# First modulation columns by float32 products with the weights stationary, and the first keys and queries summed by halves of the features

## Chip, core and metric

The program runs on one core of a Trainium2 chip. Its engines are TensorE (PE; loads of stationary operands are listed apart as PEld), VectorE (DVE), ScalarE (ACT), GpSimd (POOL) and SyncE (SP), which issues the transfers. Each engine works through its own list of instructions in order and waits on semaphores for the others. The metric is the device time of one launch in microseconds (us), lower is better. The kernel before took 2116.98 us, the median of three runs (2109.93 to 2120.24).

## What is computed

Two transformer blocks stand one behind the other. The change touches only the beginning of the first: the modulation of the inputs and the first keys and queries of its attention, cut here to this:

```python
def modulate(x, g, shift, scale):
    return rmsnorm(x, g) * (1 + scale) + shift

shift, scale, gate = jnp.split(jax.nn.silu(c) @ ada_w + ada_b, 3, axis=-1)
shift_c, scale_c, gate_c = jnp.split(jax.nn.silu(c_ctx) @ ada_w + ada_b, 3, axis=-1)
h = modulate(x, g_norm, shift[:, None], scale[:, None])
hc = modulate(ctx, g_norm, shift_c, scale_c)
y, yc = mixer_a(h, hc, ...)   # q, k, v, g = split(h @ w_in); rope; windowed attention with context keys
```

`x` has 512 tokens, `ctx` 256, both of 1024 features. `ada_w` is 1024 x 3072, and `c` and `c_ctx` are one vector each, so the modulation is a product of two rows with a large matrix: shift and scale are 2048 columns of it, for two vectors. All is float32.

## The kernel before, in words

Matrices are multiplied in float32 accuracy by splitting: `wchunk` loads a weight tile of 128 x 1024 (`raw`, 512 KB), ACT rounds it to `wH`, DVE forms the remainder `wL`, and three matmuls (H with H, L with H, H with L) stand for one product. A matmul of float32 operands that are not split is carried out by PE in two passes, and the trace counts each.

The start goes like this. `ada_stat` transposes the two condition vectors into `adast` (split, in a padded stationary operand) and `adafull` (float32, padded with zeros). `ada_cols` makes the modulation columns for one half of the features (`h`), first shift (`ada_b`), then scale (`ada_a`): `ada_chunk` sums over four weight tiles with the conditions stationary and 512 weight columns moving (tiles 0 and 2 split, 1 and 3 as float32), ACT brings the sum to `sgx`, and four products with `sel` turn its rows into columns in `tp`. In between, the six blocks of 128 tokens (two of context, four of x) are loaded (`load`), normalised and transposed (`turn`) into `xT`, features on partitions. When both halves of the columns are done, `modulate` applies them to the eight feature blocks: POOL and ACT do the context's, DVE and ACT the tokens', and both are split into X and Xc (`XH`, `XL`, `xcH`, `xcL`).

Then `attn_a` loads its constants, and `g_k(0)` and `g_q(0)` compute the first keys and queries with `gemm_T`: over the eight feature blocks k, three products each, for x (`px`, 512 columns) and context (`pc`, 256 columns). A rope, splits and copies by DMA follow, and `g_v`, the values, and the scores of the first head behind that.

The program text is written in terms of tiles; a scheduler puts each engine's instructions in order ahead of time and adds the semaphores. A tile name is reused when its last reader is done, and the transfer that refills it waits for that in SP's queue, with all that is issued behind it.

Of the kernel before, what the change touches and what calls it, by code (L numbers as in the profile page):

```python
# [270 lines left out]
class Prog:  # L271
# [193 lines left out]
    def ada_stat(self, th, ps):  # L465
        nc = self.nc
        tp = self.bank("tp")
        nc.tensor.transpose(tp[:, :16], th, self.ident[:16, :16])
        st = self.t(self.ap, [P, 8, 132], F32R, "adast", 1)
        nc.vector.memset(st.bitcast(F32), 0.0)  # L470
        v = tp[:, :16].rearrange("p (j k) -> p j k", j=2)
        for j in range(2):
            H, L = st[:, :, 3 + 64 * j], st[:, :, 35 + 64 * j]
            self.act(H, v[:, j])
            nc.vector.tensor_sub(L, v[:, j], H.bitcast(F32))
        self.adast = st
        full = self.t(self.np_, [P, 8, P], F32, "adafull", 1)
        nc.gpsimd.memset(full, 0.0)
        for j in range(2):
            nc.vector.tensor_copy(full[:, :, 64 * j], v[:, j])  # L480
        return full

    def ada_chunk(self, l, c, pm, row=0, full=None, fs=()):


        for i in range(4):
            if i in fs:
                raw = self.t(self.rp[0], [P, 1024], F32, "raw", self.rp[1])
                self.nc.sync.dma_start(raw, self.I[f"ada{l}"][c * 4 + i])
                for kk in range(2):  # L490
                    k = 2 * i + kk
                    self.mm(pm, full[:, k], raw[:, kk * 512:kk * 512 + 512], start=k == 0, stop=k == 7)
                yield
                continue
            HL = self.wchunk(self.I[f"ada{l}"][c * 4 + i])
            for kk in range(2):
                k = 2 * i + kk
                for w in range(2):
                    self.mm(pm, self.adast[:, k, 3 - row:131 - row], HL[w][:, kk * 512:kk * 512 + 512],
                            start=(k == 0 and w == 0), stop=(k == 7 and w == 1))  # L500
            yield
# [2 lines left out]
        self.ab = [self.t(self.ag if l else self.ap, [P, 2, 8], F32, f"ada_{n}{l}", 1) for n in "ab"]  # L504
        return self.ab

    def ada_cols(self, l, half, ps, tag, pool, full=None, fs=()):

        nc = self.nc
        a, b = self.ab  # L510
        hs = slice(4 * half, 4 * half + 4)
        bias = self.colv(f"ab{l}")
        for s_ in range(2):
            pm = self.bank(tag)
            yield from self.ada_chunk(l, 2 * s_ + half, pm, 0, full, fs)
            A = self.t(pool, [P, 512], F32, "sgx", 1)
            self.act(A, pm)
            tp = self.bank("tp")
            for f in range(4):
                self.mm(tp[:, 2 * f:2 * f + 2], A[:, f * P:(f + 1) * P], self.sel, start=True, stop=True)  # L520
            v = tp[:, :8].rearrange("p (k j) -> p k j", j=2)
            for j in range(2):
                bc = bias[:, 8 * s_ + 4 * half:8 * s_ + 4 * half + 4]
                if s_ == 0:
                    nc.vector.tensor_add(b[:, j, hs], v[:, :, j], bc)
                else:
                    g = self.colv(f"ng{l}")[:, hs]
                    nc.vector.tensor_add(a[:, j, hs], v[:, :, j], bc)
                    nc.vector.scalar_tensor_tensor(a[:, j, hs], a[:, j, hs], 1.0, g, op0=ALU.add, op1=ALU.mult)
            yield  # L530

    def ada_grow(self, l, c, ps, tag):
# [200 lines left out]
    def block1_(self):  # L733
# [3 lines left out]
        with ExitStack() as eb, ExitStack() as es:  # L737
# [5 lines left out]
            with ExitStack() as e2:  # L743
                tmp, ps = self.pool(e2, "A0"), None
                self.np_ = tmp
                th = self.ada_prep()
                full = self.ada_stat(th, ps)
                ab = self.ada_ab(0)
                self.rp = (tmp, 8)
                mm = "mm"  # L750
                xT = self.t(tmp, [P, 8, 768], F32, "xT", 1)

                def modulate(ks):
                    for k in ks:
                        for (j, sl, Z) in ((1, slice(0, C), Xc), (0, slice(C, C + S), X)):
                            x, a, b = xT[:, k, sl], ab[0][:, j, k:k + 1], ab[1][:, j, k:k + 1]
                            if j:
                                nc.gpsimd.tensor_scalar(x, x, a, b, op0=ALU.mult, op1=ALU.add)
                                self.act(Z[0][k], x)
                                nc.gpsimd.tensor_tensor(Z[1][k], x, Z[0][k].bitcast(F32), op=ALU.subtract)  # L760
                            else:
                                nc.vector.tensor_scalar(x, x, a, b, op0=ALU.mult, op1=ALU.add)
                                self.split(Z[0][k], Z[1][k], x)

                ga = chain(*[self.ada_cols(0, h, ps, mm, tmp, full, (1, 3)) for h in range(2)])

                def load(b):
                    xt = self.t(tmp, [P, D], F32, "x0", 6)
                    nc.sync.dma_start(xt, I["ctx"][b * P:(b + 1) * P] if b < 2 else I["x"][(b - 2) * P:(b - 1) * P])
                    return xt  # L770

                def turn(b, x):
                    r = self.row_r(x)
                    nc.vector.tensor_scalar(x, x, r, None, op0=ALU.mult)
                    for g in range(2):
                        tp = self.bank("mm", [P, 4, P])
                        for kk in range(4):
                            k = 4 * g + kk
                            nc.tensor.transpose(tp[:, kk, :], x[:, k * P:(k + 1) * P], self.ident)
                        dst = xT[:, 4 * g:4 * g + 4, b * P:(b + 1) * P]  # L780
                        if g == 0:
                            self.act(dst, tp)
                        else:
                            nc.vector.tensor_copy(dst, tp)

                run(some(ga, 1))
                for b in (0, 3):
                    xs = [load(b + i) for i in range(3)]
                    for i in range(3):
                        turn(b + i, xs[i])  # L790
                    run(some(ga, 3))
                run(ga)
                modulate(range(8))
                self.rp = None
            OT, OC = self.newO(), [self.oslot(k, F32) for k in range(8)]
            with ExitStack() as e2:
                self.attn_a(X, Xc, OT, OC, self.pool(e2, "A1"), None)
            if self.stop == "A1":
                for t in range(8):
                    self.dbg(f"OT{t}", OT[t])  # L800
# [65 lines left out]
            for b in range(4):  # L866
                self.dbg(f"x{b}", self.x[b])

    def attn_a(self, X, Xc, OT, OC, pool, ps):
        nc, I = self.nc, self.I  # L870
        rope = self.t(pool, [P, 2 * S], F32, "rope", 1)
        nc.sync.dma_start(rope, I["rope_a"])
# [4 lines left out]
        sink = self.bcast(I["a_sink"], pool, 16, "sink")  # L877
        nsink = self.t(pool, [P, 16], F32, "nsink", 1)
        nc.vector.tensor_scalar(nsink, sink, -1.0, None, op0=ALU.mult)
        V = [self.t(pool, [P, 4, P], F32R, f"V{b}", 1) for b in range(6)]  # L880
        K, Q, sg = {}, {}, {}

# [5 lines left out]
        def g_v():  # L888
            HL = [self.wchunk(I["a_v"][i]) for i in range(2)]
            for b in range(6):  # L890
# [8 lines left out]
                pv = pm[:, :256].rearrange("p (h d) -> p h d", h=4)  # L899
                self.split(V[b][:, :, 0:64], V[b][:, :, 64:128], pv)  # L900

        def g_k(pr):
            W = self.wchunk(I["a_k"][pr])
            px, pc, tk = toks()
            yield from self.gemm_T(W, tk)
            kf = self.rope(px, pool, rope, rot)
            kH = self.t(pool, [P, 768], F32R, "tH", 1)
            kL = self.t(pool, [P, 768], F32R, "tL", 1)
            self.split(kH[:, :C], kL[:, :C], pc[:, :C])
            self.split(kH[:, C:], kL[:, C:], kf)  # L910
            for e in range(2):
                k2 = self.t(pool, [P, 2, 768], F32R, "K", 2)
                for i, src in enumerate((kH, kL)):
                    for hf in range(2):
                        self.dcopy(k2[64 * hf:64 * hf + 64, i, :], src[64 * e:64 * e + 64, :])
                K[2 * pr + e] = k2
            yield

        def g_q(t):
            W = self.wchunk(I["a_q"][t])  # L920
            px, pc, tk = toks()
            yield from self.gemm_T(W, tk)
            qf = self.rope(px, pool, rope, rot)
            qH = self.t(pool, [P, 768], F32R, "tH", 1)
            qL = self.t(pool, [P, 768], F32R, "tL", 1)
# [7 lines left out]
            yield  # L933

        def g_g(t):
            W = self.wchunk(I["a_g"][t])
            px, pc, tk = toks()
            yield from self.gemm_T(W, tk)
            sg[t] = sx, sc = self.t(pool, [P, S], F32, "sgx", 1), self.t(pool, [P, C], F32, "sgc", 1)
            for ps_g, g in ((pc[:, :C], sc), (px, sx)):  # L940
                self.act(g, ps_g, AF.Tanh, scale=0.5)
                nc.vector.scalar_tensor_tensor(g, g, 1.0, ps_g, op0=ALU.add, op1=ALU.mult)
            yield
# [929 lines left out]
```

## Time and profile before

| what | us |
|---|---|
| median of three runs | 2116.98 |
| profiled execution, its own time | 2119.62 |
| its span | 2117.8 |
| PE busy in the span | 2032.1 (96%) |
| columns of the first half of the features ready | 35.3 |
| columns of the second half ready | 55.1 |
| first matmul of the first key sum | 51.87 |
| first matmul of V | 79.22 |

The span runs from the first to the last instruction of the profiled execution; 1.8 us of its time lie around it. A row of the timeline gives start, duration, engine, line and operation, then output<-inputs and their shapes, and in brackets how long the engine had been idle and what ended that. The duration of a matmul includes its way through the array, so its pace is the distance from one start to the next. PEclk is the share of TensorE's full clock (2.4 GHz) that was granted; 0.50 is 1.2 GHz.

### The profile page before, as it was taken

The page shows a single profiled execution, that of the slowest core. Times are in us where ns is not written, and L with a number is a line of the kernel's source. Part 1 is how long each engine was busy: PE and PEld are TensorE (multiplying, and loading weights), DVE is VectorE, ACT ScalarE, POOL GpSimd, SP SyncE. Part 2 cuts the span into 40 slices and gives each one's busy share as a digit, 9 for nine tenths or more (in the row PEclk, how much of TensorE's full clock was granted, in tenths as well). Part 3 has the DMA queues.
Part 4 walks back from the last instruction along what each step waited for, and adds up shares of the span by engine and source line. Part 5 has one row for each costly group of instructions (what it writes and reads, how often), then busy time and mean ns, then how long its engine had stood idle before and what let it go on. Part 6 is the DMA issues. An engine that isn't in the chain of part 4 may idle for free.

```text
span 2117.8 us, 28799 instructions
## 1 busy us (share of the span) xinstructions
PE 2032.1 (96%) x10609; PEld 1688.5 (80%) x10609; DVE 1293.2 (61%) x2491; ACT 1056.4 (50%) x2044; POOL 74.0 (3%) x162
## 2 busy tenths in 40 slices
PE   7899999998999999998999999999999999999998
PEld 4788888778788887876778888887888878888886
DVE  5588788846478886657756444423566775444323
ACT  5477677725367763555534333322466754333321
POOL 2100000000000000000000000000000000000000
PEclk9999999999999999999999999999999999999999
DMA  7344423322444332232223233232565533333332
GB/s 261 100 132 135 115 85 97 118 71 69 124 94 109 86 97 80 94 90 61 60 90 114 96 100 100 91 99 80 138 158 152 140 120 100 100 100 94 96 96 83
DMA packets 80893, 223.65 MB, mean 106 GB/s; under 512 B 13408, under 2 KB 19312, under 8 KB 80752
## 3 DMA queue, kind: packets, MB, share of 16 engines
q1 hardware_dynamic: 80752, 221.81, 34.8%
q8 instruction: 84, 1.38, 0.3%
q14 instruction: 57, 0.47, 0.1%
HBM read 176.67 MB, written 4.19 MB: 85 GB/s over the span
## 4 chain that ended last, share of the span: by engine, by line
PE 82%; DVE 7%; ACT 5%; issue 2%; DMA 2%; POOL 2%; SPq 0%; POOLq 0%; ACTq 0%; DVEq 0%
PE pj L293 33%; PE S L293 28%; PE po L293 13%; PE tp L293 2%; DVE wL L304 2%; PE tp L1305 2%; PE tp L1100 1%; ACT wH L290 1%; POOL rstd L336 1%; ACT tmp L290 1%; ACT junk L290 1%; DVE XL L584 1%; PE tp L375 1%; PE tp L1792 1%; ACT P L290 1%
## 5 line engine op out<-in xcount | busy, mean ns | idle before, releaser
L304 DVE TENSOR_TENSOR wL<-raw,wH 128x1024 fp32r<-128x1024 f32 (+2 forms) x291 | 354.1, 1221 | 465.4 <-ACT wH L290 453.2
L290 ACT ACTIVATE wH<-raw 128x1024 fp32r<-128x1024 f32 (+2 forms) x291 | 305.5, 1053 | 546.4 <-PE S L293 217.6
L293 PE MATMUL pj<-XH,wH 128*128 128x512 f32 (+1 forms) x672 | 259.9, 390 | 2.9 <-ACT tmp L290 1.5
L293 PE MATMUL pj<-XL,wH 128*128 128x512 f32 (+1 forms) x672 | 258.9, 389 | 0.1
L293 PE MATMUL pj<-XH,wL 128*128 128x512 f32 (+1 forms) x672 | 256.0, 384 | 0.5 <-DVE wL L304 0.5
L293 PE MATMUL S<-K,Q 96*128 96x384 f32 (+4 forms) x864 | 189.2, 329 | 3.9 <-ACT P L290 3.0
L293 PE MATMUL S<-XH,wH 128*128 128x512 f32 (+1 forms) x456 | 170.0, 373 | 1.0 <-ACT wH L290 1.0
L293 PE MATMUL S<-XH,wL 128*128 128x512 f32 (+1 forms) x456 | 170.1, 373 | 0.5 <-DVE wL L304 0.5
L293 PE MATMUL S<-XL,wH 128*128 128x512 f32 (+1 forms) x456 | 169.9, 373 | 0.0
L293 PEld LDWEIGHTS S<-K,Q 128*128 128x128 f32 (+1 forms) x864 | 140.7, 189 | 19.2 <-ACT P L290 7.3
L293 PEld LDWEIGHTS pj<-XH,wH 128*128 128x128 f32 x672 | 127.4, 190 | 28.5 <-ACT tmp L290 2.3
L293 PEld LDWEIGHTS pj<-XH,wL 128*128 128x128 f32 x672 | 127.0, 190 | 22.4 <-DVE wL L304 0.8
L293 PEld LDWEIGHTS pj<-XL,wH 128*128 128x128 f32 x672 | 127.1, 190 | 22.0 <-issue 0.4
L290 ACT ACTIVATE PTH<-tp 128x512 fp32r<-128x512 f32 (+2 forms) x192 | 91.3, 480 | 45.1 <-PE tp L1100 14.0
L584 DVE TENSOR_TENSOR PTL<-tp,PTH 128x512 fp32r<-128x512 f32 (+2 forms) x192 | 103.6, 543 | 10.2 <-ACT PTH L290 9.5
L293 PEld LDWEIGHTS S<-XH,wH 128*128 128x128 f32 x456 | 86.2, 189 | 16.6 <-ACT wH L290 1.7
L293 PEld LDWEIGHTS S<-XH,wL 128*128 128x128 f32 x456 | 86.2, 189 | 15.7 <-DVE wL L304 1.0
L293 PEld LDWEIGHTS S<-XL,wH 128*128 128x128 f32 x456 | 86.2, 189 | 15.2
L290 ACT ACTIVATE XH<-tp 128x512 fp32r<-128x512 f32 x128 | 75.1, 596 | 43.4 <-PE tp L375 24.0
L584 DVE TENSOR_TENSOR XL<-tp,XH 128x512 fp32r<-128x512 f32 x128 | 86.9, 686 | 10.6 <-ACT XH L290 9.5
L290 ACT ACTIVATE P<-S,nm 128x768 f32<-128x768 f32 (+1 forms) x96 | 72.5, 757 | 31.5 <-DVE nm L1018 12.4
L293 PE MATMUL po<-PTH,V 128*128 128x256 f32 (+1 forms) x224 | 78.8, 355 | 2.7 <-ACT PTH L290 2.3
(482 smaller groups left out, 4500.8 us busy)
## 6 DMA issues: line engine op xcount, KB each, us to landing
raw<-in_up SPq DMA_DIRECT2D x88, 512.0 KB, 3.5
raw<-in_ada SPq DMA_DIRECT2D x48, 512.0 KB, 4.2
raw<-in_dn SPq DMA_DIRECT2D x44, 512.0 KB, 3.5
raw<-in_o_o SPq DMA_DIRECT2D x11, 512.0 KB, 4.3
x<-in_x SPq DMA_DIRECT2D x8, 512.0 KB, 9.0
raw<-in_a_q SPq DMA_DIRECT2D x8, 512.0 KB, 4.7
raw<-in_a_g SPq DMA_DIRECT2D x8, 512.0 KB, 3.7
raw<-in_a_o SPq DMA_DIRECT2D x8, 512.0 KB, 3.6
```

Source lines behind the costliest of these rows:

```text
L290: self.nc.scalar.activation(out, in_, func, **kw)
L293: return self.nc.tensor.matmul(out, l, r, start=start, stop=stop, **kw)
L304: nc.vector.tensor_sub(L[:, :n], raw[:, :n], H[:, :n].bitcast(F32))
L336: self.nc.gpsimd.tensor_tensor(r, ms, self.c_mh[:, :n], op=ALU.pow)
L375: nc.tensor.transpose(tp[:, kk, :], xh[g][:, kk * P:(kk + 1) * P], self.ident)
L584: self.nc.vector.tensor_sub(L, src, H.bitcast(F32))
L1100: nc.tensor.transpose(tp[:, (i - i0) * P:(i - i0 + 1) * P], Ps[i][0][:, at(i) * P:(at(i) + 1) * P], self.ident)
L1305: nc.tensor.transpose(tp[:, i * P:(i + 1) * P], Ps[i][:, kb * P:(kb + 1) * P], self.ident)
L1792: nc.tensor.transpose(tp[:, (i - kb) * P:(i - kb + 1) * P], Ps[i][0][:, kb * P:(kb + 1) * P], self.ident)
```

## The change

The columns of layer 0 are no longer made by `ada_cols`. A new `ada_feat` loads the same tiles as plain float32 (those of the shift in halves, into the free tiles `OT`), makes each 128 x 128 piece of the weights the stationary operand and moves the two conditions (`cT`, two columns) past it; the sum over k stands in `tp` as columns at once. `ada_put` is the code that added bias and gain before. The six blocks of tokens are loaded ahead of all weights, and `turn` squares a whole row at a time. The constants of attention are loaded by `consts_a`, ahead of the second half's weights. The first key and query sums run as two generators, step by step: over the first four feature blocks when the first half is modulated, over the other four when the second is. The context is now modulated by ACT, not POOL. Layer 1 goes on as before.

```diff
+        cT = self.t(self.ap, [P, 8, 2], F32, "adac", 1)
+        nc.vector.tensor_copy(cT.rearrange("p k j -> p j k"), v)
...
+    def ada_feat(self, l, half, cT):
+        for s_ in range(2):
+            tp = self.bank("tp")
+            for i in range(4):
+                src = self.I[f"ada{l}"][(2 * s_ + half) * 4 + i]
+                if s_ == 0:
+                    raw = [self.t(self.op, [P, 512], F32, f"OT{2 * i + kk}", 1) for kk in range(2)]
+                    for kk in range(2):
+                        self.nc.sync.dma_start(raw[kk], src[:, kk * 512:kk * 512 + 512])
+                else:
+                    raw = self.t(self.rp[0], [P, 1024], F32, "raw", self.rp[1])
+                    self.nc.sync.dma_start(raw, src)
+                    raw = [raw[:, :512], raw[:, 512:]]
+                for kk in range(2):
+                    for f in range(4):
+                        self.mm(tp[:, 2 * f:2 * f + 2], raw[kk][:, f * P:f * P + P], cT[:, 2 * i + kk],
+                                start=i + kk + f == 0, stop=i == 3 and kk == 1, skip_group_check=True)
+                yield
+            self.ada_put(l, half, s_, tp)
+            yield
...
-                    r = self.row_r(x)
-                    nc.vector.tensor_scalar(x, x, r, None, op0=ALU.mult)
+                    ss = self.t(self.sm, [P, 2], F32, "ss2", 8)
+                    self.act(self.t(tmp, [P, D], BF16, "junkx", 1), x, AF.Square, scale=1.0 / 32.0, accum_out=ss[:, 0:1])
+                    nc.vector.tensor_scalar(ss[:, 0:1], ss[:, 0:1], EPS, None, op0=ALU.add)
+                    nc.vector.tensor_scalar(x, x, self.rstd(ss[:, 0:1]), None, op0=ALU.mult)
...
-                run(some(ga, 1))
-                for b in (0, 3):
-                    xs = [load(b + i) for i in range(3)]
-                    for i in range(3):
-                        turn(b + i, xs[i])
-                    run(some(ga, 3))
-                run(ga)
-                modulate(range(8))
+                def modulate(k):
+                    xs, zs = xT[:, k, C:], xT[:, k, :C]
+                    nc.vector.tensor_scalar(xs, xs, ab[0][:, 0, k:k + 1], ab[1][:, 0, k:k + 1], op0=ALU.mult, op1=ALU.add)
+                    self.act(zs, zs, scale=ab[0][:, 1, k:k + 1], bias=ab[1][:, 1, k:k + 1])
+                    self.split(X[0][k], X[1][k], xs)
+                    self.split(Xc[0][k], Xc[1][k], zs)
+
+                gas = [self.ada_feat(0, h, cT) for h in range(2)]
+                xs = [load(b) for b in range(6)]
+                for b in range(6):
+                    turn(b, xs[b])
+                    run(some(gas[0], 1))
+                run(gas[0])
+
+                Ws = [self.wchunk(I["a_k"][0]), self.wchunk(I["a_q"][0])]
+                consts = self.consts_a(self.pool(ea, "A0c", "right"))
+                begun = [[self.bank(kind) for _ in range(2)] for kind in ("pj", "S")]
+                gs = [self.gemm_T(W, [(X, S, px), (Xc, C, pc[:, :C])]) for W, (px, pc) in zip(Ws, begun)]
+                for h in range(2):
+                    for k in range(4):
+                        modulate(4 * h + k)
+                        for g in gs:
+                            run(some(g, 3))
+                        if h == 0:
+                            run(some(gas[1], 3 if k == 3 else 2))
+                    run(gas[1])
+                for g in gs:
+                    run(g)
...
         def g_k(pr):
-            W = self.wchunk(I["a_k"][pr])
-            px, pc, tk = toks()
-            yield from self.gemm_T(W, tk)
+            px, pc = begun[0] if pr == 0 else (yield from proj(I["a_k"][pr]))
```

PE's list in the kernel before, from the last column groups of the second half (`raw` by `adafull`) into the key sum (`pj_510`, `pj_511`):

```order
L293 MATMUL S_380<-wH_397,adast_113 128x512
L293 MATMUL S_380<-wL_398,adast_113 128x512
L293 MATMUL S_380<-raw_405,adafull_119 128x512 x2
L293 MATMUL pj_510<-XH_6_91,wH_506 128x512
L293 MATMUL pj_511<-xcH_10_95,wH_506 128x256
L293 MATMUL pj_510<-XL_8_93,wH_506 128x512
```

The key sum stood behind all products of the columns. PE's list in the changed kernel, at the end of the first half's columns (`tp_155` shift, `tp_301` scale) and the start of the key and query sums (`pj_371`, `pj_372` and `S_373`):

```order
L293 MATMUL tp_155<-adac_119,OT_56_250 128x2 x4
L293 MATMUL tp_301<-adac_119,raw_302 128x2 x8
L293 MATMUL tp_301<-adac_119,raw_312 128x2 x8
L293 MATMUL tp_301<-adac_119,raw_322 128x2 x8
L293 MATMUL tp_301<-adac_119,raw_332 128x2 x8
L293 MATMUL pj_371<-XH_6_91,wH_348 128x512
L293 MATMUL pj_371<-XL_8_93,wH_348 128x512
L293 MATMUL pj_372<-xcH_10_95,wH_348 128x256
L293 MATMUL pj_371<-XH_6_91,wL_349 128x512
L293 MATMUL S_373<-XH_6_91,wH_354 128x512
```

The key and query sums now stand behind the first half's columns alone, and the columns are made by matmuls of two moving columns. Further down in the same list, where the first half's sums go over into the second half's (`tp_393` and `tp_480` are the second half's columns, `XH_7` its features):

```order
L293 MATMUL S_374<-xcL_12_97,wH_354 128x256
L293 MATMUL S_373<-XH_6_91,wL_355 128x512
L293 MATMUL tp_393<-adac_119,OT_94_448 128x2 x4
L293 MATMUL S_374<-xcH_10_95,wL_355 128x256
L293 MATMUL tp_393<-adac_119,OT_95_449 128x2 x4
L293 MATMUL tp_480<-adac_119,raw_481 128x2 x8
L293 MATMUL tp_480<-adac_119,raw_509 128x2 x8
L293 MATMUL tp_480<-adac_119,raw_519 128x2 x8
L293 MATMUL tp_480<-adac_119,raw_529 128x2 x8
L293 MATMUL pj_371<-XH_7_92,wH_348 128x512
```

Half of the second half's column products stand among the sums over the first half, the other half between the two parts of the sums.

## Rows read from the trace of the kernel before

**Rows 1.** The page: busy time of each engine, its share of the span, instructions.
```profile
PE 2032.1 (96%) x10609; PEld 1688.5 (80%) x10609; DVE 1293.2 (61%) x2491; ACT 1056.4 (50%) x2044; POOL 74.0 (3%) x162
```
**Rows 2.** The chain that ended last: start, us, what.
```profile
35.09 0.23 DVE ada_a L528 x2
...
54.89 0.23 DVE ada_a L528 x2
```
**Rows 3.** Timeline of PE: keys, queries, and V's first matmul.
```profile
66.63 0.63 PE L293 MATMUL pj<-XL,wH 128*128 128x512 f32 x1
67.06 0.63 PE L293 MATMUL pj<-XH,wL 128*128 128x512 f32 x1
...
75.10 0.40 PE L293 MATMUL pj<-XH,wH 128*128 128x512 f32 x1
...
75.46 0.39 PE L293 MATMUL pj<-XL,wH 128*128 128x512 f32 x1
...
77.09 0.28 PE L293 MATMUL pj<-xcH,wL 128*128 128x256 f32 x1
...
79.22 0.68 PE L293 MATMUL pj<-wH,xcH 128*128 128x256 f32 x1
```
**Rows 4.** Windows: stretch and length, busy (instructions) by engine, PEclk, DMA share, GB/s.
```profile
90.00:100.00 10.00, 10.00 (x79) 9.64 (x79) 8.04 (x28) 6.85 (x19) 0.00 (x0) 1.00 0.01 2
```
**Rows 5.** Windows of PE alone: stretch and length, busy, PEclk, DMA share, GB/s.
```profile
25.00:25.50 0.50, 0.28 (x2) 1.00 1.00 401
25.50:26.00 0.50, 0.50 (x4) 0.58 1.01 401
...
29.00:29.50 0.50, 0.50 (x2) 1.00 0.75 303
```
**Rows 6.** Timeline of PE: transposes, and eight passes of two columns.
```profile
12.08 1.06 PE L779 MATMUL pj<-ident,x 128*128 128x128 f32 x4
12.94 1.91 PE L779 MATMUL S<-ident,x 128*128 128x128 f32 x8
...
16.71 0.60 PE L779 MATMUL po<-ident,x 128*128 128x128 f32 x4
17.15 0.60 PE L779 MATMUL pj<-ident,x 128*128 128x128 f32 x4
...
21.95 0.95 PE L293 MATMUL tp<-sel,sgx 128*128 128x2 f32 x8
```
**Rows 7.** Timeline of PE: matmuls of 160 columns, then of 416.
```profile
491.57 0.27 PE L293 MATMUL S<-wH,xcH 128*128 128x160 f32 x1
491.68 0.28 PE L293 MATMUL S<-wL,xcH 128*128 128x160 f32 x1
...
502.97 0.41 PE L293 MATMUL po<-wH,xcH 128*128 128x160 f32 x1
503.18 0.41 PE L293 MATMUL po<-wL,xcH 128*128 128x160 f32 x1
...
503.61 0.63 PE L293 MATMUL pj<-wH,XH 128*128 128x416 f32 x1
```
**Rows 8.** Windows of PE alone around that stretch.
```profile
497.00:498.00 1.00, 0.86 (x5) 0.50 0.67 249
...
506.00:507.00 1.00, 1.00 (x4) 0.57 0.07 16
```
**Rows 9.** Timeline of the other engines in the first 40 us.
```profile
6.23 1.06 ACT L290 ACTIVATE wH<-raw 128x1024 fp32r<-128x1024 f32 x1 [1.96 <-DMA raw<-in_ada]
...
8.26 0.63 ACT L290 ACTIVATE junk<-x 128x512 bf16<-128x512 f32 x1
8.79 0.19 ACT L290 ACTIVATION_READ_ACCUMULATOR junk<-x 128x1 f32 x1
...
9.31 0.55 POOL L336 TENSOR_TENSOR rstd<-ss,mh 128x1 f32<-128x1 f32 x1 [7.63 <-DVE adast L475]
9.90 0.75 DVE L774 TENSOR_SCALAR x<-x,rstd 128x1024 f32<-128x1024 f32 x1 [0.44 <-POOL rstd L336]
12.32 0.60 ACT L290 ACTIVATE xT<-S 128x512 f32<-128x512 f32 x1 [1.08 <-PE S L779]
...
35.49 1.55 DVE L762 TENSOR_SCALAR xT<-xT,ada_a,ada_b 128x512 f32<-128x512 f32 x3
36.96 1.21 DVE L304 TENSOR_TENSOR wL<-raw,wH 128x1024 fp32r<-128x1024 f32 x1
```
**Rows 10.** The tile `sgx`, first 70 us: count, ns min/median/max, first and last start, forms.
```profile
L293 PE MATMUL tp<-sel,sgx x32: 165/251/272, 22.0 to 54.6; 128*128 128x2 f32 x32
```

More of the change, by code (lines that the diff above doesn't have):

```diff
@@ L476, in ada_stat, with ada_chunk @@
         self.adast = st
[L477 to L483, printed above, removed]
-        for i in range(4):
[L487 to L494, printed above, removed]
+        cT = self.t(self.ap, [P, 8, 2], F32, "adac", 1)
+        nc.vector.tensor_copy(cT.rearrange("p k j -> p j k"), v)
+        return cT
+    def ada_feat(self, l, half, cT):
[18 more added lines that the diff above has]
+            yield
+    def ada_chunk(self, l, c, pm, row=0):
+        for i in range(4):
             HL = self.wchunk(self.I[f"ada{l}"][c * 4 + i])
@@ L505, in ada_ab, with ada_put @@
         return self.ab
-    def ada_cols(self, l, half, ps, tag, pool, full=None, fs=()):
+    def ada_put(self, l, half, s_, tp):
         nc = self.nc
@@ L511, in ada_cols @@
         hs = slice(4 * half, 4 * half + 4)
-        bias = self.colv(f"ab{l}")
+        v = tp[:, :8].rearrange("p (k j) -> p k j", j=2)
+        for j in range(2):
+            bc = self.colv(f"ab{l}")[:, 8 * s_ + 4 * half:8 * s_ + 4 * half + 4]
+            if s_ == 0:
+                nc.vector.tensor_add(b[:, j, hs], v[:, :, j], bc)
+            else:
+                g = self.colv(f"ng{l}")[:, hs]
+                nc.vector.tensor_add(a[:, j, hs], v[:, :, j], bc)
+                nc.vector.scalar_tensor_tensor(a[:, j, hs], a[:, j, hs], 1.0, g, op0=ALU.add, op1=ALU.mult)
+    def ada_cols(self, l, half, ps, tag, pool):
         for s_ in range(2):
             pm = self.bank(tag)
-            yield from self.ada_chunk(l, 2 * s_ + half, pm, 0, full, fs)
+            yield from self.ada_chunk(l, 2 * s_ + half, pm)
             A = self.t(pool, [P, 512], F32, "sgx", 1)
@@ L520, in ada_cols @@
                 self.mm(tp[:, 2 * f:2 * f + 2], A[:, f * P:(f + 1) * P], self.sel, start=True, stop=True)
[L521 to L529, printed above, removed]
+            self.ada_put(l, half, s_, tp)
             yield
@@ L746, in block1_ @@
                 th = self.ada_prep()
-                full = self.ada_stat(th, ps)
+                self.rp = (tmp, 8)
+                cT = self.ada_stat(th, ps)
                 ab = self.ada_ab(0)
-                self.rp = (tmp, 8)
-                mm = "mm"
                 xT = self.t(tmp, [P, 8, 768], F32, "xT", 1)
[L753 to L765, printed above, removed]
                 def load(b):
@@ L796, in block1_ @@
             with ExitStack() as e2:
-                self.attn_a(X, Xc, OT, OC, self.pool(e2, "A1"), None)
+                self.attn_a(X, Xc, OT, OC, self.pool(e2, "A1"), None, consts, begun)
             if self.stop == "A1":
@@ L867, in block1_, with consts_a @@
                 self.dbg(f"x{b}", self.x[b])
-    def attn_a(self, X, Xc, OT, OC, pool, ps):
+    def consts_a(self, pool):
         nc, I = self.nc, self.I
@@ L879, in attn_a @@
         nc.vector.tensor_scalar(nsink, sink, -1.0, None, op0=ALU.mult)
+        return rope, rot, mask, sink, nsink
+    def attn_a(self, X, Xc, OT, OC, pool, ps, consts, begun):
+        nc, I = self.nc, self.I
+        rope, rot, mask, sink, nsink = consts
         V = [self.t(pool, [P, 4, P], F32R, f"V{b}", 1) for b in range(6)]
@@ L900, in g_v, with proj @@
                 self.split(V[b][:, :, 0:64], V[b][:, :, 64:128], pv)
+        def proj(W):
+            px, pc, tk = toks()
+            yield from self.gemm_T(self.wchunk(W), tk)
+            return px, pc
         def g_k(pr):
-            W = self.wchunk(I["a_k"][pr])
-            px, pc, tk = toks()
-            yield from self.gemm_T(W, tk)
+            px, pc = begun[0] if pr == 0 else (yield from proj(I["a_k"][pr]))
             kf = self.rope(px, pool, rope, rot)
@@ L919, in g_q @@
         def g_q(t):
-            W = self.wchunk(I["a_q"][t])
-            px, pc, tk = toks()
-            yield from self.gemm_T(W, tk)
+            px, pc = begun[1] if t == 0 else (yield from proj(I["a_q"][t]))
             qf = self.rope(px, pool, rope, rot)
@@ L935, in g_g @@
         def g_g(t):
-            W = self.wchunk(I["a_g"][t])
-            px, pc, tk = toks()
-            yield from self.gemm_T(W, tk)
+            px, pc = yield from proj(I["a_g"][t])
             sg[t] = sx, sc = self.t(pool, [P, S], F32, "sgx", 1), self.t(pool, [P, C], F32, "sgc", 1)
```

## The prediction

> **What bounds the kernel now.** I read the page first: PE is busy for 96% of the span [rows 1], so a change near the start counts only as far as it lets PE reach its later work sooner or later. The chain of waits shows where the start is spent: the modulation columns of the first half of the features are ready at 35.3 us, those of the second half at 55.1 [rows 2]. After them come the sums of the first keys and queries. The timeline has their last matmul at 77.09 and the first matmul of V at 79.22 [rows 3], and from 90 to 100 PE has no idle time [rows 4]. Behind the first V matmul both programs issue the same work, and V's 144 matmuls give the ropes and copies of keys and queries time to finish. So the time changes by as much as the first V matmul moves. I call that moment M: 79.2 before.
>
> What the change puts ahead of M depends on the clock, so I looked at that next. It stood at full speed until 25.5 us and then fell to half until 29 [rows 5]. What PE had done just before the fall was transposes, eight passes of two columns [rows 6], and waits: it was busy for 0.28 of the last 0.50 us. The second place lies at 497 to 506 [rows 7, 8]: PE busy without a gap, with matmuls of 160 columns whose pace is not their streaming but the weight load; the clock stood at 0.50 all that time and rose only after matmuls of 416 columns. These two places decide the forecast.
>
> **What goes, what comes.** Before, each of four column groups took two weight tiles by eight matmuls of split weights and two by four float32 ones. Their eight splits each on ACT and DVE go (1.06 and 1.21 us [rows 9]), as do four evacuations and the two-column products behind them. Now all 128 products are float32 with the weights stationary and two columns moving; each is two passes, 256 in all. The trace has this operation, eight passes in 0.95 us at full clock [rows 6], one of them 0.25 [rows 10]: (0.95 - 0.25)/7 = 0.10 us a pass. At half clock the trace never shows it. From below its pace is 0.10, if the load does not follow the clock; from above 0.21, the pace of the 160-column matmuls at half clock (502.97 to 503.18) against 0.11 at full (491.57 to 491.68) [rows 7]. I take 0.21: both are paced by a 128-column weight load. So the 256 passes cost 26 us at full clock and 54 at half.
>
> *Until the first half is ready.* The first transfer in the queue is now x, not a weight tile. The one there before had landed by 6.23 [rows 9]; at 401 GB/s [rows 5] a 0.52 MB tile follows every 1.31 us, so the sixth x is there at 12.8. Two squares of 512 with their read (0.63 + 0.19 each [rows 9]) become one of 1024, not shown: at least 1.06 + 0.19 = 1.25 (the 1024-wide copy), at most 2 x 0.82 = 1.64; I take 1.25, since only the length changes. From a square's end to the first transpose takes 1.7 us (adds, the power on POOL 0.55, the scaling 0.75 [rows 9], and the steps between). So transposes begin at about 9.2. ACT has six squares and six 0.60 evacuations [rows 9], 11.1 us from 6.3, and the last square ends near 16.9: the last x is ready at 18.5. On PE a group of four transposes costs 0.86 at half clock and 0.44 at full [rows 6]. The first three x fill it to 14.4, the fourth is ready at 15.5. From there come 6 groups and 32 passes: all at half clock 5.2 + 6.7 = 11.9, until 27.4; all at full, held by the last x, 20.2. Before, transposes alone brought the clock up (half pace at 12.08, full at 16.71), so some run at full clock: I take 26. Then 96 passes in a row: 20.2 at half clock, 46.2. Four small DVE steps of 0.23 [rows 2] make it T = 47, against 35.3 before.
>
> *The sums over the first half, with the second half's first 64 passes between them.* DVE's modulation (1.55 for three [rows 9]), XH (0.60, as an evacuation of that size) and, queued behind it on ACT, the copy of the key weights (1.06) stand ahead of the first matmul: T + 2.3; the first product with wL waits for wL (1.21) to T + 4.2. PE has 24 pairs (a 512 and a 256 matmul), 0.35 a pair (75.10 to 75.46 [rows 3]): 8.3 us at full clock, double at half (66.63 to 67.06 is 0.43 for a 512 [rows 3]). 3.7 us of it (11 matmuls of 512, 10 of 256) come before the first two-column group in PE's order. They begin at half clock; dense work brought it back after 3.4 us in the fall at 25.6 [rows 5], so they end at about T + 9. The rest, 4.6 + 6.4 = 11.0 us at full clock, alternates dense matmuls and passes. If it falls again as at 25.6, 3.4 of it run at full and 7.6 take 15.2: T + 27.7. A mixed stretch like this is not in the trace; bounds are 11.0 and 22.
>
> *The last 64 passes* run by themselves, because the second half's matmuls in PE's order stand behind them: 13.4 at half clock, 6.4 at full; T + 41. Columns, modulation and XH: 2.4 us in which PE has nothing queued. The second half's 24 pairs: 8.3 + 1.7 for the clock's return. With 0.5 for the first rope M = T + 54 = 101.
>
> The other edits: the constants' loads move ahead in SP's queue past the second half's weights and are no longer late; POOL loses the context's modulation, and ACT and DVE take it over, which have room once those splits are gone. The loads of the second half wait in SP's queue for PE's passes to free their tiles, and V's weights are queued behind; at 401 GB/s and 54 us of PE work none of them comes late. I set these at nothing; they would cost up to 2 us if V's tiles were late.
>
> Sum: 101 - 79.2 = +22 us on the profiled execution's 2119.6, which stands 2.6 above the median; on the median 2139.
>
> The Trainium skill, TensorE: Matmul & The Clock Gate, section "What's actually happening", says that the half clock is the default state and activity releases it; the trace agrees at both places [rows 5, 8], and this speaks against the change.
>
> **Rivals.** *The clock stays at full* through the passes, because PE is never idle. For it: in the trace two-column passes came in eights only, and the fall at 25.6 had waits beside them. Against it: the 160-column stretch had none [rows 8]. Then T = 20.2 + 9.6 + 0.9 = 30.7, T + 9 less 1.5 for the sums begun warm, 11.0, 6.4, 2.4, 8.3 and 0.5 give M = 66.8: -12, 2105. This one is faster: it decides from the point at which fewer than some 40% of the passes run at half clock.
>
> *The pace of the load does not follow the clock*: 0.10 a pass throughout, only streaming is halved. 15.5 + 5.2 + 3.2 + 9.6 + 0.9 = 34.4 = T; T + 9, then about 14, 6.4, 2.4, 10, 0.5: M = 77, -2, 2115. The 160-column rows speak against it. The same page's section on LDWEIGHTS gives a load time from the columns alone, with no clock in it; by that rule this rival would hold, but the rows at 491 and 503 differ by a factor of two [rows 7].
>
> *Passes at half clock, mixed sums at full*: dense matmuls between the passes hold the clock. T = 47, T + 9 + 11.0, the 64 passes 3.4 us at full and the other 30 at half 6.3, 2.4, 10, 0.5: M = 90, +10, 2127.
>
> *All at half clock up to the second half's sums*: mixed 22, first 3.7 us doubled with no recovery (T + 11.6), T = 48.4: M = 108, +29, 2146.
>
> **How the numbers follow.** Forecast +22: 0.50. All at half clock: 0.10. Mixed sums at full: 0.14. Load not following the clock: 0.08. Clock at full: 0.18. The range leaves out most of the last and the far end above the fourth: 2110 to 2150; the forecast's own range is 2131 to 2144 (the mixed stretch's bounds, and the start's 27.4). A measurement of this kernel can tell about 0.5%, 10.6 us, from no change. Slower by more: 0.50 + 0.10 + 0.06 of the mixed case = 0.66. Within: 0.08 + 0.08 = 0.16. Faster: 0.18.
>
> **What would show it.** In the profile after: a granted clock near 0.5 between about 16 and 50 us and again in the 64 passes before the second half; passes 0.21 apart; columns of the first half at about 47; the first V matmul near 101. If the clock reads 1.00 there and the passes stand 0.10 apart, the first rival holds; half clock with 0.10 apart is the second. A first V matmul below 79 makes the forecast wrong in sign. If M is near 101 and the time is not up by some 20 us, my claim that work behind M just shifts is wrong.

## The result, and the profile after

The changed kernel takes 2129.98 us (median of 4 runs, 2128.66 to 2133.06), the kernel before 2118.05 in the runs beside it: ratio 1.0065, 95% interval 1.0036 to 1.0095, slower by 12 us from median to median. Its profiled execution took 2128.7, 9.1 more than the one of before. I forecast 2139, so the direction and the place were right and the size was not: of the +22 announced a little over half came.

The page of the change: span, busy time by engine, and TensorE's clock in 40 slices of 53 us.
```profile
span 2126.9 us, 29056 instructions
...
PE 2050.2 (96%) x10769; PEld 1719.1 (81%) x10769; DVE 1281.2 (60%) x2490; ACT 1048.4 (49%) x2028; POOL 54.5 (3%) x145
...
PEclk7899999999999999998999999999999999999999
```
PE is as full as before [rows 1], with more busy time. The first two slices, 106 us, now have a low clock; of the others one alone reads 8, and nothing else on the page stands out.

Windows of PE at the start: window, length, PE's busy time and instructions, granted clock, DMA share and rate.
```profile
20.00:22.00 2.00, 2.00 (x18) 0.83 1.03 412
22.00:24.00 2.00, 2.00 (x12) 0.50 1.02 408
...
50.00:52.00 2.00, 2.00 (x7) 0.50 0.00 0
52.00:54.00 2.00, 2.00 (x16) 0.99 0.03 8
...
62.00:64.00 2.00, 2.00 (x18) 1.00 0.00 0
...
66.00:68.00 2.00, 2.00 (x11) 0.50 0.00 0
...
82.00:84.00 2.00, 2.00 (x11) 0.81 0.00 0
```
PE is busy throughout these windows, and for two stretches, 21.3 to 52.1 and 65.7 to 82.8, the clock is at its lower level, 0.50 of full. One wait of PE lies in each, 2.7 and 1.7 us long, but both falls came while PE was busy: at 65.7 it had been so without a gap since 47.2. Before, the clock was low three times for 3.4 us each, not only at 25.6 [rows 5] but again at 46.1 and 66.5 (stretch and length, PE, PEld, DVE, ACT, POOL, granted clock, DMA):
```profile
46.00:48.00 2.00, 2.00 (x4) 0.95 (x3) 2.00 (x2) 1.32 (x2) 0.00 (x0) 0.51 0.00 0
...
68.00:70.00 2.00, 2.00 (x6) 1.25 (x4) 0.00 (x0) 0.00 (x0) 0.00 (x0) 0.51 0.92 344
```
Up to some 14 us the reading says nothing: it is 1.00 from the start in every trace here, while the transposes at 12.08 still stand at twice their later distance [rows 6].

The timeline of PE: start, length of the group, engine and line, output<-input, shapes and count. The rows of two columns are the new passes; the last row is M, the first matmul of V.
```profile
16.49 0.95 PE L293 MATMUL tp<-adac,OT 128*128 128x2 f32 x8
...
22.55 6.83 PE L293 MATMUL tp<-adac,OT 128*128 128x2 f32 x32
29.23 13.79 PE L293 MATMUL tp<-adac,raw 128*128 128x2 f32 x64
45.74 0.79 PE L293 MATMUL pj<-XH,wH 128*128 128x512 f32 x1 [2.71 <-ACT wH L290]
...
52.67 0.95 PE L293 MATMUL tp<-adac,OT 128*128 128x2 f32 x8
...
63.55 0.95 PE L293 MATMUL tp<-adac,OT 128*128 128x2 f32 x8
64.37 12.58 PE L293 MATMUL tp<-adac,raw 128*128 128x2 f32 x64
78.64 0.79 PE L293 MATMUL pj<-XH,wH 128*128 128x512 f32 x1 [1.69 <-ACT XH L290]
89.97 0.68 PE L293 MATMUL pj<-wH,xcH 128*128 128x256 f32 x1
```
The columns of the two halves are ready when DVE's last small steps end:
```profile
43.26 0.23 DVE L531 SCALAR_TENSOR_TENSOR ada_a<-ada_a,cols 128x4 f32<-128x4 f32 x2
...
77.18 0.24 DVE L531 SCALAR_TENSOR_TENSOR ada_a<-ada_a,cols 128x4 f32<-128x4 f32 x2
```
At 43.5 and 77.4, where before had 35.3 and 55.1 [rows 2]. M moved from 79.22 [rows 3] to 89.97, +10.75, and the span by +9.1: work behind M shifted, and 1.6 us were given back on the way. In the ten kernels below, too, the span moves by as much as M, from -11.9 to +39.6 us, to within 5 us. A pass stands 0.10 from the next at full clock (eight in 0.95) and 13.79/64 = 0.215 at half.

### The profile page after: what moved, and what is told of

Same layout as the page of the kernel before. It is cut to its first block, busy times and chain, and to the rows that moved or that the text cites. A ratio compares the mean times of both kernels' runs of the same rounds, so it can differ in the third digit from the quotient of the medians.

```text
span 2126.9 us, 29056 instructions
## 1 busy us (share of the span) xinstructions
PE 2050.2 (96%) x10769; PEld 1719.1 (81%) x10769; DVE 1281.2 (60%) x2490; ACT 1048.4 (49%) x2028; POOL 54.5 (3%) x145
## 4 chain that ended last, share of the span: by engine, by line
PE 84%; DVE 7%; ACT 5%; issue 2%; POOL 1%; DMA 1%; SPq 0%; POOLq 0%; ACTq 0%; DVEq 0%
PE pj L293 33%; PE S L293 29%; PE po L293 13%; PE tp L293 4%; PE tp L1331 1%; PE tp L1126 1%; DVE wL L304 1%; POOL rstd L336 1%; DVE XL L598 1%; ACT tmp L290 1%; ACT wH L290 1%; PE tp L1818 1%; ACT junk L290 1%; ACT P L290 1%; PE tp L375 1%
## 5 line engine op out<-in xcount | busy, mean ns | idle before, releaser
L304 DVE TENSOR_TENSOR wL<-raw,wH 128x1024 fp32r<-128x1024 f32 (+2 forms) x283 | 343.4, 1217 | 459.6 <-ACT wH L290 447.0
L290 ACT ACTIVATE wH<-raw 128x1024 fp32r<-128x1024 f32 (+2 forms) x283 | 297.2, 1053 | 531.7 <-PE pj L293 196.5
L293 PEld LDWEIGHTS S<-XH,wL 128*128 128x128 f32 x448 | 84.6, 189 | 14.4
L290 ACT ACTIVATE P<-S,nm 128x768 f32<-128x768 f32 (+1 forms) x96 | 72.4, 757 | 29.6 <-DVE nm L1319 10.5
```

Of the source, the lines that this page charges most:

```text
L290: self.nc.scalar.activation(out, in_, func, **kw)
L293: return self.nc.tensor.matmul(out, l, r, start=start, stop=stop, **kw)
L304: nc.vector.tensor_sub(L[:, :n], raw[:, :n], H[:, :n].bitcast(F32))
```

## The experiments

The runs of before beside the first four had a median of 2116.5, beside the next four 2114.6, beside the last two 2117.5. M, the windows and the timelines are of one profiled execution of each kernel.

**Is it the clock, and what holds it?** The same number of passes, but 128 columns move instead of 2; 126 of them are zeros.
```
-        cT = self.t(self.ap, [P, 8, 2], F32, "adac", 1)
+        cT = [self.oslot(k, F32)[:, :128] for k in range(8)]   # zeros beyond 2 columns
...
-   self.mm(tp[:, 2 * f:2 * f + 2], raw[kk][:, f * P:f * P + P], cT[:, 2 * i + kk], ...
+   self.mm(tp[:, w * f:w * f + w], raw[kk][:, f * P:f * P + P], cT[2 * i + kk][:, :w], ...   # w = 128
```


> Every column product moves 128 columns (two conditions and 126 zeros) past the same stationary weights, in place of two; products, loads of weights and transfers are the same in number, the scheduler shifts some neighbours. Theory A (the two-column passes let the clock fall, and half clock doubles the pace of the weight loads): granted clock 1.00 from 20 to 80 us, passes 0.11 apart, columns of the first half at about 33 us (43.5 in the change), first V matmul near 70 (90), time some 19 us below the change and 8 below the kernel before, about 2110. Rival B (a load of unsplit float32 weights takes 0.2 us whatever the clock, or the clock falls anyway): passes 0.21 apart, first V matmul near 90, time 2129 or more.

2109.48 us (7 runs), ratio to before 0.9961 (0.9947 to 0.9975): some 20 us under the change, by adding zeros. Timeline, and two of the windows:
```profile
26.08 7.31 PE L293 MATMUL tp<-OC,raw 128*128 128x128 f32 x64
...
52.59 5.52 PE L293 MATMUL tp<-OC,raw 128*128 128x128 f32 x48
...
69.41 0.68 PE L293 MATMUL pj<-wH,xcH 128*128 128x256 f32 x1
```
```profile
20.00:24.00 4.00, 4.00 (x38) 1.00 1.03 410
...
64.00:68.00 4.00, 4.00 (x25) 1.00 0.00 0
```
64 passes take 7.31 us where the same 64 took 13.79. M is 20.6 earlier than in the change (in the fastest of the seven runs, 2105.73). With 128 columns the clock read 1.00 in every window of 4 us from 8 to 104 us, with 2 it fell, and PE was busy in both: the loss of the change is the clock's.

**Each half by itself.** The same edit for the passes of one half only (w = 128 and 2, then 2 and 128).

> 128 moving columns for the products of the first half of the features alone, two for the second half. Theory A: the stretch from 21 to 43 us runs at full clock and is 10 us shorter, the last 64 passes still fall to half clock; first V matmul near 78, about 12 us below the change. Rival B: no difference from the change.

> 128 moving columns for the second half alone. Theory A: passes of the first half at 0.21 as in the change, columns of the first half at 43.5; the last 64 passes take 7 us in place of 12.6 and the sums behind them start at full clock: first V matmul near 82, about 7 us below the change. Rival B: no difference from the change.

First half wide: 2122.16 (10 runs), ratio 1.0015 (1.0003 to 1.0028), M = 85.91 where 78 was expected. Second half wide: 2124.4 (10 runs), 1.0025 (1.0011 to 1.004), M = 86.53 where 82 was expected. Each edit helps, neither as much as I said; the second's interval overlaps that of the change (1.0036 to 1.0095), and there M, 3.4 us earlier, is the better sign. In the second, the same program has both paces:
```profile
32.95 13.79 PE L293 MATMUL tp<-OC,raw 128*128 128x2 f32 x64
...
69.70 5.52 PE L293 MATMUL tp<-OC,raw 128*128 128x128 f32 x48
```
Its first half ended 3.7 us later than in the change, and the clock fell at 17.5 instead of 21.3. In the first, the columns came at 34.0, about as expected, and then the mixed stretch fell, which in the change it had not. Windows of PE, and the passes just ahead of the fall:
```profile
40.00:42.00 2.00, 2.00 (x16) 1.00 0.41 158
42.00:46.00 4.00, 4.00 (x18) 0.50 0.00 1
...
58.00:62.00 4.00, 4.00 (x17) 0.50 0.00 0
```
```profile
38.35 1.84 PE L293 MATMUL tp<-OC,OT 128*128 128x2 f32 x16
...
40.72 0.95 PE L293 MATMUL tp<-OC,OT 128*128 128x2 f32 x8
```
24 passes stood there with three dense matmuls (512 or 256 moving columns) between them. So a stretch of passes and sums that began at full clock can fall. From 42 on passes and sums alternate for 20 us, passes for 9.7 of the 17.9 from 44.05 to 61.97, and the clock stays at 0.50.

**The order alone.** The columns by split weights as before, with x first and the sums by halves as in the change.
```
...
-  gas = [self.ada_feat(0, h, cT) for h in range(2)]
+  gas = [self.ada_cols(0, h, ps, "po", tmp, cT, (1, 3)) for h in range(2)]   # before's columns
...
```


> The columns are made as in the kernel before (conditions stationary, 512 weight columns moving, half of the tiles split), with x first and the sums by halves as in the change. Theory A: the clock stays up, columns of the first half at about 32 us, first V matmul between 67 and 72, time about 10 us below the kernel before, 2108. Rival C (the order is the loss: x ahead of the weights, sums that wait for each half): no faster than the change, 2129 or more.

2117.77 (12 runs), ratio 1.0005 (0.9994 to 1.0016): the order neither loses nor brings the 10 us that I gave it; M = 77.40, where I expected 67 to 72 and before had 79.22. Two windows of PE:
```profile
20.00:24.00 4.00, 3.61 (x8) 0.60 0.97 359
...
64.00:68.00 4.00, 2.54 (x8) 0.52 0.30 116
```
It waits for splits and evacuations, and the clock is low around these waits: 16.4 to 23.2, 40.2 to 43.7 and 64.1 to 71.0, 17 us in all, so theory A's clock that stays up did not come about. The order alone does not lose, so the loss came with the float32 products.

**Halves at full clock.** 128 columns, and all passes ahead of all sums.
```
+                run(gas[1])
                 for h in range(2):
                     for k in range(4):
                         modulate(4 * h + k)
                         for g in gs:
                             run(some(g, 3))
-                        if h == 0:
-                            run(some(gas[1], 3 if k == 3 else 2))
-                    run(gas[1])
```


> The kernel with 128 moving columns in every column product, and now all 256 passes ahead of the sums (the second half's passes no longer between the first half's sums, so the sums run in one piece). Theory A (the time follows the first V matmul M, and once the clock stays at full the order of passes and sums is worth little): first half's columns at 33.5 as there, the second half's 14 us later at 48, then 48 pairs of 0.35 = 16.8 and some 4 us of modulation, split and first weights: M about 69, as with halves (69.4), ratio to before 0.996. Theory B (the halves are worth what they hide, the wait for modulation and splits of 2 to 4 us): M 72 to 73, ratio 0.998. Theory C (a row of 256 passes without dense matmuls between lets the clock fall even at 128 columns): 0.21 a pass in the second half, M above 80.

2105.5 (5 runs), 0.9947 (0.9935 to 0.9959): the lowest median of all, 9 us under the median of before beside it and 11 by the ratio. The sums by halves show no gain here: M is 2.1 earlier without them, and the two intervals overlap. A window from the row of passes ahead of the sums, and M:
```profile
44.00:48.00 4.00, 4.00 (x38) 1.00 0.45 131
```
```profile
67.28 0.68 PE L293 MATMUL pj<-wH,xcH 128*128 128x256 f32 x1
```
In all windows of 4 us from 8 to 120 the clock was 1.00. Two matmuls of the sums still stood between the halves' passes, but the second half's 128 followed without anything between, 35.67 to 49.88: they do not let the clock fall, and theory C is out.

**Half as many columns.** As the first experiment, with 64 columns moving.

> As the kernel with 128 moving columns in every column product (62 or 126 of them zeros that are not used), but 64 columns. Theory A (it is what the passes themselves stream that keeps the clock up): either 64 columns do, then passes are 0.11 apart throughout and M is about 69, ratio 0.996; or they do not, then 0.21 apart for most of the first 128 passes and M near 90, ratio 1.006; in between the clock would be up in part. Theory B (it is something else in that kernel, such as where the columns lie in SBUF or the other layout of the results): 64 columns have the same layout and so the same time as 128, M 69 and the passes at full clock for certain. So only a time above 2113 tells against B; a time of 2109 leaves both.

2113.51 (10 runs, 2109.2 to 2125.3), 0.9994 (0.9978 to 1.0011), in between. The profiled execution is the longest of the ten, and in it both happen:
```profile
32.65 13.86 PE L293 MATMUL tp<-OC,raw 128*128 128x64 f32 x64
...
69.80 5.47 PE L293 MATMUL tp<-OC,raw 128*128 128x64 f32 x48
```
The first half ran at half clock from 18 on, the second at full, and M came at 89.77. What the shorter executions had is not in a trace. The layout is that of 128 columns, so it is not the layout that gave the gain (theory B falls).

**No passes among the first sums.** The change without the two lines `if h == 0: run(some(gas[1], ...))`.

> The change, with none of the second half's passes between the first half's sums: all 128 of them follow in one row. Theory A (dense matmuls between passes of two columns hold the clock, passes alone let it fall): first half's columns at 43.5 as in the change, first sums until about 59; then 128 passes, some 30 at full clock (3.2 us) and 98 at 0.215 (21 us), until 83; 2.4 and 10 and 0.5 for the second half's sums: M about 96, 6 us later than the change's 90, ratio to before 1.009. Theory B (the clock came back at 52 for a reason of its own, not for the dense matmuls between, and fell again at 66 likewise): the passes' share at full clock is what it was, M 89 to 91, ratio 1.0065.

2132.9 (6 runs), 1.0076 (1.0062 to 1.009); M = 93.33, 3.4 later than in the change, between the theories.
```profile
55.80 10.52 PE L293 MATMUL tp<-adac,OT 128*128 128x2 f32 x64
66.18 13.79 PE L293 MATMUL tp<-adac,raw 128*128 128x2 f32 x64
...
93.33 0.68 PE L293 MATMUL pj<-wH,xcH 128*128 128x256 f32 x1
```
The 64 passes that stood among the sums take 10.52 us now (64 at 0.10 would be 6.5): the clock fell at 59.2, while they ran, and not after them, as theory A says. Between dense matmuls, in the change, the same passes had left it at 1.00. Part of the loss comes back, since the clock had returned at 49.0 in the first sums and not at 52. The timed difference to the change is too small for these runs.

**Added dense work.** A matmul of 512 columns on the constant columns behind every eight passes.
```
+   self.mm(self.bank("po"), self.adast[:, 0, :P], self.adast[:, :4, :P], start=True, stop=True)
```


> The change, with one 512-column matmul of one-pass type that computes nothing needed behind every eight passes of two columns: 32 matmuls more, 0.23 us each at full clock, 7.4 us of added TensorE work. Theory A (dense matmuls between passes hold the clock): passes 0.10 apart with the fillers, first half's columns at about 37 (15.5 + 128 x 0.105 and 16 x 0.23, and the rest of the transposes), the last 64 passes 8.5 us and no 3 us for the clock's return: M about 78, ratio about 1.000, so faster than the change in spite of more work. Theory B (only the width of the pass itself matters, or the clock falls whatever stands between): half clock as in the change, 32 x 0.43 more: M 100 to 104, ratio 1.012.

2148.96 (4 runs), 1.0154 (1.0141 to 1.0167); M = 107.23. It was not the experiment I had in mind: the added matmuls wait for no weight tile, so all 32 ran ahead of the first half's columns, and each took longer than I had put: 0.80 us at half clock in a row of five (40.64 to 44.62), where a sum's matmul of 512 columns takes 0.43 [rows 3]. Still, a stretch of it tells something:
```profile
37.37 3.41 PE L293 MATMUL tp<-adac,raw 128*128 128x2 f32 x16
40.64 4.19 PE L293 MATMUL po<-adast 128*128 128x512 f32 x5
44.62 3.41 PE L293 MATMUL tp<-adac,raw 128*128 128x2 f32 x16
```
```profile
40.00:44.00 4.00, 3.80 (x8) 0.50 0.44 130
...
72.00:76.00 4.00, 4.00 (x32) 1.00 0.00 0
```
From 24.4 to 57.4 the added matmuls had more than half of the time, and the clock stayed at 0.50. So dense work between passes does not always bring the clock back; but these matmuls move their columns at about half the rate of the sums, so the run does not show what as much of the sums' own work would have done. Later, from 69 to 81, the first sums with eights of passes among them ran at 1.00.

**The same mixture in sixteens.** Of each pair of tiles of the second half the later one is used first; the schedule then puts sixteen passes between eight or nine matmuls.
```
-   for kk in range(2):
+   for n, kk in enumerate((1, 0) if half else (0, 1)):
...
```


> The change, but of each pair of weight tiles of the second half the one that arrives last is used first, so that the passes come between the first half's sums in sixteens with eight or nine dense matmuls between, not in eights with four or five; the work and its sum are the same. Theory A (it is how finely passes and dense matmuls alternate that held the clock in the change's mixed stretch): the clock falls in the mixed stretch, as in the run with 128 columns in the first half only, where it fell after a group of sixteen: 4 to 8 us more, M 94 to 98, ratio to before 1.009. Theory B (the share of dense work decides, the grain does not matter): mixed stretch at 1.00 and M 89 to 91, ratio 1.0065.

2126.64 (6 runs), 1.0047 (1.0029 to 1.0065); M = 86.71. Theory A missed: no fall in the mixed stretch.
```profile
24.00:26.00 2.00, 2.00 (x13) 0.62 1.02 397
...
50.00:54.00 4.00, 4.00 (x33) 1.00 0.01 4
54.00:58.00 4.00, 4.00 (x33) 1.00 0.00 0
...
63.00:65.00 2.00, 2.00 (x11) 0.50 0.00 0
```
Passes had 6.8 of the 10.9 us from 50.20 to 61.09, in sixteens, and the clock stayed at 1.00. With the first half wide the same kind of mixture, with a smaller share of passes, stayed at 0.50 from 42 to 62. One difference is what came before: here sums alone, which had brought the clock back at 48.4; there a fall, behind 24 passes with only three dense matmuls between them. The runs do not tell which of these two counts, the level at the entry or how closely the passes stood. The first half of this kernel is the change's, instruction by instruction on PE, yet the clock fell at 24.5 and not at 21.3, and the columns came 2.9 us earlier: that is most of the 3.3 us in M.

**Added dense work behind each eight.** The added matmul now reads the weight tile of its passes, in float32.
```
+   self.mm(self.bank("po"), raw[kk][:, :P], raw[kk], start=True, stop=True)
```


> The change, with one 512-column float32 matmul on the same weight tile behind each eight passes, whose result nothing needs: 32 more, two passes each, 0.42 us at full clock by the run with added matmuls before this one (there they ran ahead of their passes; here they need the tile that the passes need). 13.4 us of added TensorE work at full clock. Theory A (dense work between eights holds the clock in any stretch, as in the mixed one): passes 0.10 apart; T = 33.4 + 16 x 0.42 = 40, mixed stretch 8 x 0.42 longer, the last 64 passes 10.1 for 12.6, no clock's return 3: M about 84, ratio 1.004, less than the change. Theory B (0.42 us of dense work to 0.81 of passes is too little, the mixed stretch had more than one to one): half clock as in the change, 32 x 0.84 = 27 less what falls in the mixed stretch at full (8 x 0.42): M 110 to 114, ratio 1.016.

2159.49 (4 runs, 2148.14 to 2163.02), 1.0192 (1.016 to 1.0225); M = 118.82, above both. An added matmul cost 0.94 us at full clock (two passes of 0.47, where a sum's matmul of 512 columns takes 0.23), not 0.42, so no time here tests a theory. Nor had the change's mixed stretch more than one to one, as I wrote in theory B: its sums had 5.2 us beside 6.5 of passes. The clock:
```profile
28.00:32.00 4.00, 4.00 (x15) 0.50 0.55 192
...
96.00:100.00 4.00, 4.00 (x30) 1.00 0.00 0
100.00:104.00 4.00, 4.00 (x26) 1.00 0.00 0
104.00:106.00 2.00, 2.00 (x11) 0.78 0.00 0
```
Passes and added matmuls in turn (with transposes in the first stretch, sums in the second) ran at 0.50 from 16.4 to 40.3 and at 1.00 from 81.2 to 105.1, so either level can last through a mixture for over 20 us. It need not: between these stretches the clock fell at 43.7, 50.5 and 74.4 and rose at 47.1 and 64.1, and it fell again at 105.1, all in mixtures of this kind.

## Why the prediction was right in sign and too large

*What bounds it.* Right: the start decides. M +10.75, span +9.1, and to within 5 us so in all runs.

*The pace of a pass at half clock*, taken as 0.21 between bounds of 0.10 and 0.21: right, 0.215. With it the rival in which the load does not follow the clock falls. The Trainium skill, TensorE: Matmul & The Clock Gate, section "LDWEIGHTS (loading the stationary operand)", has no clock in its load time; these passes, paced by a 128-column load, differ by a factor of two, and the measurement decides.

*The clock falls while PE is never idle.* Right, and the point on which the sign hung; the kernel with 128 columns shows it by undoing it. But the row that I took for it did not show it: the 160-column stretch ran on at half clock without a gap [rows 8], yet the fall ahead of it, at 496.7, came in a wait, so "the 160-column stretch had none" holds only behind the fall.
```profile
496.00:497.00 1.00, 0.00 (x0) 0.81 0.83 283
```
In the whole trace of before the clock falls eleven times, each time with a wait of PE in the 4 us ahead; that it falls without one too was a right guess, not a reading. The Trainium skill, the same page, section "Why this matters for your kernels", warns of idle gaps between bursts of matmuls; here PE had none from 22.6 to 42.8 and ran at 0.50.

*T, the first half's columns, forecast 47, came at 43.5.* The 96 passes in a row took 20.3 (20.2 forecast), but began at 22.55 and not at 26: the later transposes and the first passes ran at full pace, from about 14.4 until the fall at 21.3. In three executions with this same start the fall came at 21.3 (the change), 21.7 (no passes among the sums) and 24.5 (sixteens), so 3 us of T can't be forecast from the rows.

*The step that failed: "If it falls again as at 25.6, 3.4 of it run at full and 7.6 take 15.2: T + 27.7."* The mixed stretch did not fall. It ended at T + 20.9: 6.8 us of the 11 by which M was too late (3.5 is T; 0.7 the last passes, columns and sums). I took a fall beside transposes and waits [rows 5, 6] for the model of a stretch whose other half are matmuls of 512 and 256 columns without a wait. The 3.4 us that I let run at full first is the length of the low stretch there; no row of before shows how long passes hold the clock. The runs show in its place that in the change the sums alone, 45.74 to 52, restored the clock and the mixed stretch then kept it at 1.00 for all its 11.7 us, 6.5 of them passes; the same passes without sums between them lost it after 3.4 us (55.80 to 59.2). That is the stretch of the rival "passes at half clock, mixed sums at full", to which I gave 0.14. That its M of 90 is met to 0.1 is luck: its T was 3.5 us too late, its last passes 2.9 and its mixed stretch 0.7 too short.

Why the stretch kept its clock is open. With sixteens it kept 1.00, and with the first half wide 0.50 for 18 us, as if such a stretch kept the level with which it is entered; but the second had itself begun at 1.00 and fallen, and with float32 matmuls behind each eight the clock both fell and rose in mixtures. No run changed the entry alone.

*Last passes, columns, second sums*, forecast 13.4, 2.4 and 10.5: 12.6, 1.7 and 11.3. *The edits set at nothing* are no more than the small rest. Not in the forecast: the changed order with the old products gains nothing (2117.77, at half clock for 17 us), while wide passes, which keep the clock up, reached 2109.5 with halves and 2105.5 without, near the 2105 of my first rival.

## What to carry to other kernels

A stream of matmuls whose pace is the weight load and which move few columns can leave TensorE 100% busy and its clock at half; price such a stretch at both levels before trading splits and evacuations for it. Here moving 128 columns, mostly zeros, cost hardly any pace and gave some 20 us back. For a mixed stretch, do not take over the clock of another stretch: here mixtures ran at either level, and both outcomes belong in the range.

## What the runs showed of the hardware

A stream of passes of two columns lost the clock while PE was busy without a gap (the fall at 65.7 in the change, PE busy since 47.2), and 128 columns kept it in the same place. At full clock a float32 pass of 128 columns stands 0.11 from the next (7.31/64), one of 2 columns 0.10: the columns up to 128 are nearly free beside the load. At half clock 64 columns and 2 take the same (13.86 and 13.79 for 64). The moment of the fall differed between executions of the same instructions by 3 us (21.3 to 24.5), enough to move these kernels' times by as much.
